# Key-1 quarters for the last add, the store and the maximum of a gate chunk

## The chip, the cores and the metric

One NeuronCore of a Trainium2 chip runs the whole program. The metric is the device time of one execution in microseconds, the median of several runs. The engines are named as in the profile: PE (matrix products), PEld (its weight loads), DVE (vector), ACT (scalar, which also has a DMA queue of its own, shown as ACTq), POOL (gather DMAs here), SP (the queue that loads weights).

## The reference, cut to what matters

Two transformer layers on 256 tokens of width 2048. The change lies in the first layer's expert stage: each token picks, for each of 8 heads, 16 of 16384 experts by two keys of 128, and mixes them.

```python
v1, i1 = lax.top_k(s1, 16)            # key 1: best 16 of 128, per token and head
v2, i2 = lax.top_k(s2, 16)            # key 2
cand = v1[..., :, None] + v2[..., None, :]
sc, sel = lax.top_k(cand.reshape(T, 8, 256), 16)
eidx = i1 * 128 + i2                  # of the selected pairs: 128 experts a token
gates = softmax(sc)
act = gelu(einsum('cd,ced->ce', x, u_emb[eidx]))
out = einsum('ce,ced->cd', gates * act, v_emb[eidx])
```

The kernel computes `act` densely for all 16384 experts, spreads the gates into a dense table by key 1, key 2 and token, and then reads the rows of both that some token uses.

## The kernel before, in words

**The dense products.** `linear` (L140) computes 512 output columns for all 256 tokens in two PSUM banks named `lin`. `wtile` loads 128x2048 weights (`raw`, three buffers, SP queue), `halves` splits each half of 1024 columns into a high part on ACT (`whi`, L123) and a rest on DVE (`wlo`, L124), four buffers of each, and `mm3` multiplies high by high (L134), rest by high (L135) and high by low (L136). A half feeds 12 matrix products. The stretch of interest is the product with `u`: 32 calls of `linear`, each followed by Gelu on ACT (`act`, L783), eight transposes on PE (L790), a copy (`actT`, L792) and two stores of 256 KB on ACT's queue (L794).

**The gate table.** Beside it runs the gate work, four chunks of 64 tokens (loop at L652). For each pair of tokens there are one-hot rows on DVE (L657 to L661) and ACT (L666), two products into a PSUM bank `sc` (L667, two banks), a copy of the high part on ACT (`gh`, L672) and an add on DVE into `gsb` (L673). `gsb` is 128 (key 2, partitions) x 128 (key 1) x 64 (tokens), and there is one buffer. When a chunk is full, ACT's queue issues two stores, each of 64 keys 1 (2 MB in runs of 64 floats, L676), and DVE takes the maximum over the 64 tokens in one instruction (L678, L681), which says what experts are used. The next chunk's first add must wait until the stores have landed.

**The order.** A scheduler places every engine's instructions in a fixed order by priorities. The gate work has a low priority, except what stands under `prompt()`, which has that of the dense products. After the four chunks come the places and lists (L700 to L774), still beside the product with `u`, and then the stage that gathers rows of `v` by these lists.

Of the kernel before, what the change touches and what calls it, by code (L numbers as in the profile page):

```python
# [12 lines left out]
F32 = mybir.dt.float32  # L13
# [5 lines left out]
ALU = mybir.AluOpType  # L19
AX = mybir.AxisListType  # L20

P = 128
# [34 lines left out]
def tile_kernel(ctx: ExitStack, tc: tile.TileContext, A, out):  # L57
    nc = tc.nc
    V, S, G, TE = nc.vector, nc.scalar, nc.gpsimd, nc.tensor

    def pool(name, bufs=1, space=None, stack=ctx):
        kw = {"space": space} if space is not None else {}
        return stack.enter_context(tc.tile_pool(name=name, bufs=bufs, **kw))
# [8 lines left out]
    def bank(name="bk"):  # L72
        tg, nb = {"lin": ("lin", 3), "tp": ("tp", 2), "sc": ("sc", 2), "z": ("sc", 2)}.get(name, ("x", 1))
        return pp.tile([P, 512], F32, tag=tg, name=name, bufs=nb)
# [286 lines left out]
    for c in range(2):  # L361
# [7 lines left out]
        for j in range(0, 4, 2):  # L369
# [9 lines left out]
            for jj in range(2):  # L379
                xh, xl = yl(4 * c + j + jj)  # L380
                split(y[:, jj, :], xh, xl, vcol("g_lru", 4 * c + j + jj))
                for tt in range(2):
# [4 lines left out]
                        axis=AX.X, op=ALU.add)  # L387
# [84 lines left out]
    for c in range(2):  # L472
        ps = linear(WIN, 5 + c, xt, range(4))
        qsb = []
        for tt in range(2):
            q = ap_.tile([P, 8, 64], F32, tag="qsb", name="qsb")
# [50 lines left out]
    AGv = AG.rearrange("(i p) (e a t) -> p i e a t", p=P, e=2, a=2)  # L527
# [22 lines left out]
    for n in range(4):  # L550
        ps = linear(A["w_pq"], n, x1t, range(4))
        qs = []
        for tt in range(2):
            q = rq.tile([P, 512], F32, tag="rq", name="rq", bufs=2)
# [22 lines left out]
    @contextmanager  # L577
    def prompt():

        low[0] = tc.cur_priority  # L580
        tc.cur_priority = low0
        yield
        tc.cur_priority = low[0]
# [9 lines left out]
    for tt in range(2):  # L593
# [23 lines left out]
        for half, op, c in ((0, ALU.logical_shift_right, 4), (1, ALU.bitwise_and, 15)):  # L617
# [5 lines left out]
            for h in range(8):  # L623
# [4 lines left out]
                                op=ALU.mult)  # L628
# [15 lines left out]
    gp = pool("gates", 1, stack=r3p)  # L644


    used = rp.tile([P, 2, P], F32, tag="used", name="used")
# [3 lines left out]
    for c in range(4):  # L651
        gsb = gp.tile([P, P, 64], F32, tag="gsb", name="gsb", bufs=1)  # L652
        for t0 in range(0, 64, 4):
            t = 64 * c + t0
            io = iota.unsqueeze(1).to_broadcast([P, 4, P])
            oh = gp.tile([P, 4, P], F32R, tag="oh2", name="oh2", bufs=2)
            V.tensor_tensor(oh, io, i2T[:, t:t + 4].unsqueeze(2).to_broadcast([P, 4, P]), op=ALU.is_equal)  # L657
            o1 = gp.tile([P, 4, P], F32, tag="oh1", name="oh1", bufs=2)
            V.tensor_tensor(o1, io, i1T[:, t:t + 4].unsqueeze(2).to_broadcast([P, 4, P]), op=ALU.is_equal)
            og = gp.tile([P, 4, 2, P], F32R, tag="og", name="og", bufs=2)  # L660
            V.tensor_tensor(og[:, :, 1, :], o1, gT[:, t:t + 4].unsqueeze(2).to_broadcast([P, 4, P]), op=ALU.mult)  # L661
            for k0 in range(0, 4, 2):
                ps = bank("sc")
                for k in range(k0, k0 + 2):
                    with prompt():
                        S.activation(og[:, k, 0, :], o1[:, k, :], AF.Copy, scale=gTh[:, t + k:t + k + 1])  # L666
                        TE.matmul(ps[:, (k - k0) * T:(k - k0 + 1) * T], lhsT=oh[:, k, :],  # L667
                                  rhs=og[:, k].rearrange("p a b -> p (a b)"), start=True, stop=True)
                pv = ps.rearrange("p (k m i) -> p m i k", k=2, m=2)
                gh = gp.tile([P, P, 2], F32, tag="gh", name="gh", bufs=2)  # L670
                with prompt():
                    S.activation(gh, pv[:, 0], AF.Copy)  # L672
                    V.tensor_tensor(gsb[:, :, t0 + k0:t0 + k0 + 2], gh, pv[:, 1], op=ALU.add)  # L673
        h, t0 = c // 2, c % 2 * 64
        for e in range(0, P, 64):
            S.dma_start(AGv[:, 1 + e:65 + e, h, 1, t0:t0 + 64], gsb[:, e:e + 64, :])  # L676
        if t0 == 0:
            V.tensor_reduce(used[:, h, :], gsb, axis=AX.X, op=ALU.max)  # L678
        else:
            um = gp.tile([P, P], F32, tag="um", name="um")  # L680
            V.tensor_reduce(um, gsb, axis=AX.X, op=ALU.max)  # L681
            V.tensor_tensor(used[:, h, :], used[:, h, :], um, op=ALU.max)
    r3p.close()

# [179 lines left out]
    last = []  # L864
# [14 lines left out]
    with tc.If(more > 0):  # L879
        with tc.For_i(0, P, 1) as k:  # L880
# [10 lines left out]
            for c in range(4):  # L891
# [5 lines left out]
                for tt in range(2):  # L897
# [5 lines left out]
                    op=ALU.mult)  # L903
# [102 lines left out]
    for h0 in (0, 4):  # L1006
        for tt in range(2):
            s = mq.tile([P, 4, T], F32, tag="s2", name="s2", bufs=2)
            for j in range(2):
# [3 lines left out]
                for hh in range(2):  # L1013
                    h = h0 + 2 * j + hh
# [80 lines left out]
    for h0 in (0, 4):  # L1095
        for tt in range(2):
# [4 lines left out]
            for e in range(2):  # L1101
                ps = bank("sc")
                b = slice(64 * e, 64 * e + 64)
                for j in range(2):
                    h = h0 + 2 * j + e
# [172 lines left out]
```

## Time and profile before

| | us |
|---|---|
| median of 3 runs | 3051.96 |
| lowest, highest run | 3048.44, 3052.6 |
| the profiled execution, its own time | 3049.11 |
| its span, first to last instruction | 3047.3 |
| PE busy in the span | 2970.9 (97%) |
| DVE busy | 2002.0 (66%) |
| ACT busy | 1576.9 (52%) |

PE is the engine whose queue is the program: what it does not wait for costs nothing. The times in the trace are counted from the start of the span. A row that begins with a time is one instruction, or several alike merged, with its start, its duration, and in brackets how long the engine sat idle before it and what ended that. ACTq rows are DMA issues, and their duration is the time that ACT's queue was held by the issue, not the time of the transfer. "issue" as a releaser means that the engine waited for nothing that the profile shows as work.

### The profile page before, as it was taken

The page shows a single profiled execution, that of the slowest core. Times are in us where ns is not written, and L with a number is a line of the kernel's source. Part 1 is how long each engine was busy: PE and PEld are TensorE (multiplying, and loading weights), DVE is VectorE, ACT ScalarE, POOL GpSimd, SP SyncE. Part 2 cuts the span into 40 slices and gives each one's busy share as a digit, 9 for nine tenths or more (in the row PEclk, how much of TensorE's full clock was granted, in tenths as well). Part 3 has the DMA queues.
Part 4 walks back from the last instruction along what each step waited for, and adds up shares of the span by engine and source line. Part 5 has one row for each costly group of instructions (what it writes and reads, how often), then busy time and mean ns, then how long its engine had stood idle before and what let it go on. Part 6 is the DMA issues. An engine that isn't in the chain of part 4 may idle for free. (4 is left out here: it accounts for less than half of the span.)

```text
span 3047.3 us, 36250 instructions
## 1 busy us (share of the span) xinstructions
PE 2970.9 (97%) x13729; PEld 2443.6 (80%) x13729; DVE 2002.0 (66%) x2944; ACT 1576.9 (52%) x2221; POOL 271.0 (9%) x232
## 2 busy tenths in 40 slices
PE   9999999998988999899999999999999999999999
PEld 7887888887877778678887788778888888888887
DVE  6885789877766769467777756664655454445454
ACT  6754545565655645455565555544444444344443
POOL 0000000000000000477662000000000000000000
PEclk9999999999999999999999999999999999999999
DMA  6442546656567575688886454554655555555554
GB/s 231 155 174 98 180 166 210 215 196 219 189 205 217 181 232 184 226 327 325 333 322 250 173 183 169 205 179 169 242 193 187 194 185 188 193 193 194 190 190 159
DMA packets 197168, 626.26 MB, mean 206 GB/s; under 512 B 82688, under 2 KB 116096, under 8 KB 129664
## 3 DMA queue, kind: packets, MB, share of 16 engines
q1 hardware_dynamic: 73728, 460.55, 42.8%
q0 software_dynamic: 20784, 124.79, 11.1%
q10 hardware_dynamic: 102480, 38.58, 4.8%
q8 instruction: 108, 1.77, 0.2%
q14 instruction: 68, 0.56, 0.1%
HBM read 583.77 MB, written 40.11 MB: 205 GB/s over the span
## 5 line engine op out<-in xcount | busy, mean ns | idle before, releaser
L124 DVE TENSOR_TENSOR wlo<-raw,whi 128x1024 fp32r<-128x1024 f32 (+1 forms) x972 | 1181.4, 1221 | 772.5 <-ACT whi L123 759.8
L123 ACT ACTIVATE whi<-raw 128x1024 fp32r<-128x1024 f32 (+1 forms) x972 | 1023.4, 1057 | 1087.0 <-PE lin L136 901.6
L134 PE MATMUL lin<-whi,x1th 128*128 128x512 f32 x1152 | 451.5, 399 | 25.4 <-ACT whi L123 25.4
L135 PE MATMUL lin<-wlo,x1th 128*128 128x512 f32 x1152 | 457.9, 397 | 6.2 <-DVE wlo L124 6.2
L136 PE MATMUL lin<-whi,x1tl 128*128 128x512 f32 x1152 | 457.1, 397 | 0.0
L134 PEld LDWEIGHTS lin<-whi,x1th 128*128 128x128 f32 x1152 | 219.6, 191 | 70.0 <-ACT whi L123 27.7
L136 PE MATMUL lin<-whi,x3tl 128*128 128x512 f32 x704 | 274.9, 391 | 0.0
L135 PE MATMUL lin<-wlo,x3th 128*128 128x512 f32 x704 | 274.2, 389 | 0.0
L134 PE MATMUL lin<-whi,x3th 128*128 128x512 f32 x704 | 269.5, 390 | 0.0
L135 PEld LDWEIGHTS lin<-wlo,x1th 128*128 128x128 f32 x1152 | 220.4, 191 | 51.3 <-DVE wlo L124 8.5
L136 PEld LDWEIGHTS lin<-whi,x1tl 128*128 128x128 f32 x1152 | 220.1, 191 | 43.5
L135 PE MATMUL lin<-wlo,y1th 128*128 128x512 f32 x512 | 200.7, 393 | 0.8 <-DVE wlo L124 0.8
L134 PE MATMUL lin<-whi,y1th 128*128 128x512 f32 x512 | 199.4, 395 | 1.7 <-ACT y1th L159 1.2
L136 PE MATMUL lin<-whi,y1tl 128*128 128x512 f32 x512 | 198.5, 393 | 0.8 <-DVE y1tl L160 0.8
L135 PEld LDWEIGHTS lin<-wlo,x3th 128*128 128x128 f32 x704 | 132.2, 188 | 27.3
L136 PEld LDWEIGHTS lin<-whi,x3tl 128*128 128x128 f32 x704 | 132.2, 188 | 27.1
L134 PEld LDWEIGHTS lin<-whi,x3th 128*128 128x128 f32 x704 | 132.2, 188 | 26.9
L130 POOL DMA_INDIRECT vag<-ag,idg x102 | 134.2, 1315 | 53.7 <-issue 26.5
L136 PE MATMUL lin<-whi,at 128*128 128x512 f32 x352 | 137.2, 390 | 0.0
L135 PE MATMUL lin<-wlo,at 128*128 128x512 f32 x352 | 137.0, 389 | 0.0
L134 PE MATMUL lin<-whi,at 128*128 128x512 f32 x352 | 135.5, 389 | 0.0
L134 PEld LDWEIGHTS lin<-whi,y1th 128*128 128x128 f32 x512 | 96.2, 188 | 22.4 <-ACT y1th L159 1.8
(440 smaller groups left out, 4750.1 us busy)
## 6 DMA issues: line engine op xcount, KB each, us to landing
raw<-in_u_dram SPq DMA_DIRECT2D x128, 1024.0 KB, 4.8
raw<-in_w_in_dram SPq DMA_DIRECT2D x91, 1024.0 KB, 4.8
raw<-in_w_gu_dram SPq DMA_DIRECT2D x88, 1024.0 KB, 4.8
raw<-in_w_dn_dram SPq DMA_DIRECT2D x44, 1024.0 KB, 4.7
raw<-in_w_out_dram SPq DMA_DIRECT2D x16, 1024.0 KB, 4.8
raw<-in_w_pq_dram SPq DMA_DIRECT2D x16, 1024.0 KB, 4.8
ag<-actT ACTq DMA_DIRECT2D x64, 256.0 KB, 3.0
ag<-gsb ACTq DMA_DIRECT2D x8, 2048.0 KB, 15.5
```

Source lines behind the costliest of these rows:

```text
L123: S.activation(h[:, q], r, AF.Copy)
L124: V.tensor_sub(l[:, q], r, h[:, q].bitcast(F32))
L130: G.indirect_dma_start(out=dst, out_offset=None, in_=src, in_offset=bass.IndirectOffsetOnAxis(ap=rows, axis=0))
L134: TE.matmul(ps, lhsT=xh, rhs=wh, start=start, stop=False)
L135: TE.matmul(ps, lhsT=xh, rhs=wl, start=False, stop=False)
L136: TE.matmul(ps, lhsT=xl, rhs=wh, start=False, stop=stop)
```

## The change

For the last two tokens of a chunk the add (until now one instruction of 128 keys under `prompt()`) is put off until after the loop and cut into four quarters of 32 keys 1. Behind each quarter's add stand, in the program, the store of that quarter (1 MB, all 64 tokens) and the maximum of that quarter, into `um`. In the chunks whose maximum went straight into `used`, a copy from `um` now follows. So a chunk has four adds of 64 columns, four stores and four maxima where it had one add of 256 columns, two stores and one maximum. The quarter adds, the stores and the maxima have the low priority.

```diff
                 with prompt():
                     S.activation(gh, pv[:, 0], AF.Copy)
-                    V.tensor_tensor(gsb[:, :, t0 + k0:t0 + k0 + 2], gh, pv[:, 1], op=ALU.add)
+                    if not last:
+                        V.tensor_tensor(gsb[:, :, t0 + k0:t0 + k0 + 2], gh, pv[:, 1], op=ALU.add)
...
-        for e in range(0, P, 64):
-            S.dma_start(AGv[:, 1 + e:65 + e, h, 1, t0:t0 + 64], gsb[:, e:e + 64, :])
+        um = gp.tile([P, P], F32, tag="um", name="um")
+        for e in range(0, P, 32):
+            q = slice(e, e + 32)
+            V.tensor_tensor(gsb[:, q, 62:64], gh[:, q], pv[:, 1, q], op=ALU.add)
+            S.dma_start(AGv[:, 1 + e:33 + e, h, 1, t0:t0 + 64], gsb[:, q, :])
+            V.tensor_reduce(um[:, q], gsb[:, q, :], axis=AX.X, op=ALU.max)
         if t0 == 0:
-            V.tensor_reduce(used[:, h, :], gsb, axis=AX.X, op=ALU.max)
+            V.tensor_copy(used[:, h, :], um)
         else:
-            um = gp.tile([P, P], F32, tag="um", name="um")
-            V.tensor_reduce(um, gsb, axis=AX.X, op=ALU.max)
             V.tensor_tensor(used[:, h, :], used[:, h, :], um, op=ALU.max)
```

The scheduler makes a new order from this. ACT at the end of the first chunk, before:

```order
L123 ACTIVATE whi<-raw 128x1024
L672 ACTIVATE gh<-sc 128x256
L676 DMA ag<-gsb 128x64x64 x2
L123 ACTIVATE whi<-raw 128x1024 x2
L672 ACTIVATE gh<-sc 128x256
L666 ACTIVATE og<-oh_4516,gTh 128x128 x4
L123 ACTIVATE whi<-raw 128x1024 x2
```

and now:

```order
L123 ACTIVATE whi<-raw 128x1024
L673 ACTIVATE gh<-sc 128x256
L682 DMA ag<-gsb 128x32x64 x4
L123 ACTIVATE whi<-raw 128x1024 x2
L673 ACTIVATE gh<-sc 128x256
L666 ACTIVATE og<-oh_4526,gTh 128x128 x4
L123 ACTIVATE whi<-raw 128x1024 x2
```

Two issues became four at one place, with nothing between them. DVE there likewise has its four adds in a row, a one-hot row, and then its four maxima in a row: the adds and maxima do not alternate. In the second chunk the four stores stand together too, where before the second store stood behind two stores of `actT` and one `whi`.

ACT at the end of the third chunk, before:

```order
L123 ACTIVATE whi<-raw 128x1024
L676 DMA ag<-gsb 128x64x64 x2
L123 ACTIVATE whi<-raw 128x1024
L672 ACTIVATE gh<-sc 128x256
L666 ACTIVATE og<-oh_5230,gTh 128x128 x4
L792 ACTIVATE actT<-tp 128x512 x2
L123 ACTIVATE whi<-raw 128x1024
L794 DMA ag<-actT 128x4x128 x2
L123 ACTIVATE whi<-raw 128x1024 x2
```

and now:

```order
L682 DMA ag<-gsb 128x32x64
L799 DMA ag<-actT 128x4x128 x2
L682 DMA ag<-gsb 128x32x64
L123 ACTIVATE whi<-raw 128x1024
L682 DMA ag<-gsb 128x32x64 x2
L123 ACTIVATE whi<-raw 128x1024
L673 ACTIVATE gh<-sc 128x256
L666 ACTIVATE og<-oh_5258,gTh 128x128 x4
L123 ACTIVATE whi<-raw 128x1024 x2
```

The pair of `actT` stores moved from behind the chunk's stores into their middle, and one `whi` stands between the second and the third quarter. In the fourth chunk the first quarter stands alone, then `act` and one `whi`, then three quarters.

PE at the beginning of the second chunk, before and now (a run of four `sc` products serves four tokens and fills two banks; `lin` is the dense product):

```order
L136 MATMUL lin<-whi,x1tl 128x512
L667 MATMUL sc<-og,oh_4492 128x256 x4
L667 MATMUL sc<-og,oh_4514 128x256 x4
L134 MATMUL lin<-whi,x1th 128x512 x2
L135 MATMUL lin<-wlo,x1th 128x512
```

```order
L136 MATMUL lin<-whi,x1tl 128x512
L667 MATMUL sc<-og,oh_4502 128x256 x4
L134 MATMUL lin<-whi,x1th 128x512 x2
L667 MATMUL sc<-og,oh_4524 128x256 x2
L135 MATMUL lin<-wlo,x1th 128x512
```

The second chunk began with eight such products in one run and now begins with four, the next ones spread out. The third chunk began with eight and now begins with twelve; the fourth began with twelve and now begins with eight.

## Rows read from the trace of the kernel before

**Rows 1.** Waits of PE from 700 to 1110: total us, times, longest.
```profile
PE lin L134 <- ACT whi L123: 25.4, 6, 7.6
PE lin L135 <- DVE wlo L124: 6.2, 5, 1.7
PE sc L667 <- DVE gsb L673: 5.9, 4, 1.7
```
**Rows 2.** Windows: length, busy us of PE, PEld, DVE, ACT, POOL (instructions), PEclk, DMA, GB/s.
```profile
640.00:690.00 50.00, 50.00 (x244) 42.02 (x243) 37.94 (x54) 34.38 (x70) 0.00 (x0) 1.00 0.54 190
829.00:872.00 43.00, 31.93 (x126) 25.19 (x126) 27.29 (x27) 17.43 (x32) 0.00 (x0) 0.84 0.79 220
```
**Rows 3.** Timeline of ACT and its DMA queue at the ends of the four chunks.
```profile
697.54 0.38 ACTq L676 DMA_DIRECT2D ag<-gsb  x1
697.95 9.98 ACTq L676 DMA_DIRECT2D ag<-gsb  x1
...
829.28 9.66 ACTq L794 DMA_DIRECT2D ag<-actT  x1
839.63 1.06 ACT L123 ACTIVATE whi<-raw 128x1024 fp32r<-128x1024 f32 x1 [9.57 <-issue]
...
960.07 9.37 ACTq L676 DMA_DIRECT2D ag<-gsb  x2
973.03 10.42 ACTq L794 DMA_DIRECT2D ag<-actT  x1
...
1087.12 11.12 ACTq L676 DMA_DIRECT2D ag<-gsb  x2
```
**Rows 4.** Timeline of PE there: the first products after a stop.
```profile
710.03 0.69 PE L134 MATMUL lin<-whi,x1th 128*128 128x512 f32 x1 [5.01 <-ACT whi L123]
...
844.07 0.80 PE L134 MATMUL lin<-whi,x1th 128*128 128x512 f32 x1 [7.55 <-ACT whi L123]
...
970.43 0.50 PE L135 MATMUL lin<-wlo,x1th 128*128 128x512 f32 x1 [1.26 <-DVE wlo L124]
985.22 0.79 PE L134 MATMUL lin<-whi,x1th 128*128 128x512 f32 x1 [6.79 <-ACT whi L123]
...
1100.35 0.79 PE L134 MATMUL lin<-whi,x1th 128*128 128x512 f32 x1 [5.28 <-ACT whi L123]
```
**Rows 5.** Windows behind two stops and inside a run of gate products.
```profile
710.10:713.00 2.90, 2.90 (x7) 2.31 (x8) 2.90 (x5) 2.26 (x6) 0.00 (x0) 0.51 0.96 218
844.10:849.80 5.70, 5.70 (x14) 4.44 (x15) 2.12 (x4) 0.64 (x1) 0.00 (x0) 0.50 1.14 348
731.80:737.40 5.60, 3.86 (x9) 2.79 (x10) 5.60 (x8) 4.50 (x9) 0.00 (x0) 0.70 0.17 37
```
**Rows 6.** Timeline of PE at the beginning of the second and the fourth chunk.
```profile
728.56 0.63 PE L667 MATMUL sc<-og,oh 128*128 128x256 f32 x4
730.91 0.83 PE L667 MATMUL sc<-og,oh 128*128 128x256 f32 x4 [1.72 <-DVE gsb L673]
734.26 0.80 PE L135 MATMUL lin<-wlo,x1th 128*128 128x512 f32 x1 [1.73 <-DVE wlo L124]
...
996.06 0.83 PE L667 MATMUL sc<-og,oh 128*128 128x256 f32 x4 [0.76 <-DVE gsb L673]
998.61 0.83 PE L667 MATMUL sc<-og,oh 128*128 128x256 f32 x4 [1.72 <-DVE gsb L673]
```
**Rows 7.** Timeline of DVE: last add and maximum of a chunk, next chunk's first add.
```profile
697.10 0.41 DVE L673 TENSOR_TENSOR gsb<-gh,sc 128x256 f32<-128x256 f32 x1
698.03 8.68 DVE L678 TENSOR_REDUCE used<-gsb 128x128 f32<-128x8192 f32 x1
...
726.59 0.75 DVE L673 TENSOR_TENSOR gsb<-gh,sc 128x256 f32<-128x256 f32 x2 [6.54 <-DMA ag<-gsb]
```
**Rows 8.** Timeline of ACT's queue: a pair of small stores with nothing ahead.
```profile
723.61 1.33 ACTq L794 DMA_DIRECT2D ag<-actT  x2
```
**Rows 9.** Timeline of POOL: the second gather of rows of `v`.
```profile
1237.51 0.94 POOL L130 DMA_INDIRECT raw<-in_v_dram,idv  x1 [12.24 <-DVE wlo L124]
```

More of the change, by code (lines that the diff above doesn't have):

```diff
@@ L670, in tile_kernel @@
                 gh = gp.tile([P, P, 2], F32, tag="gh", name="gh", bufs=2)
+                last = t0 + k0 == 62
                 with prompt():
                     S.activation(gh, pv[:, 0], AF.Copy)
-                    V.tensor_tensor(gsb[:, :, t0 + k0:t0 + k0 + 2], gh, pv[:, 1], op=ALU.add)
+                    if not last:
+                        V.tensor_tensor(gsb[:, :, t0 + k0:t0 + k0 + 2], gh, pv[:, 1], op=ALU.add)
         h, t0 = c // 2, c % 2 * 64
-        for e in range(0, P, 64):
-            S.dma_start(AGv[:, 1 + e:65 + e, h, 1, t0:t0 + 64], gsb[:, e:e + 64, :])
+        um = gp.tile([P, P], F32, tag="um", name="um")
[4 more added lines that the diff above has]
+            V.tensor_reduce(um[:, q], gsb[:, q, :], axis=AX.X, op=ALU.max)
         if t0 == 0:
-            V.tensor_reduce(used[:, h, :], gsb, axis=AX.X, op=ALU.max)
+            V.tensor_copy(used[:, h, :], um)
         else:
-            um = gp.tile([P, P], F32, tag="um", name="um")
-            V.tensor_reduce(um, gsb, axis=AX.X, op=ALU.max)
             V.tensor_tensor(used[:, h, :], used[:, h, :], um, op=ALU.max)
```

## The prediction

> **What bounds the kernel now.** I read first the waits of PE, since PE is busy for nearly the whole span. Between 700 and 1110, where the chunks of the gate table end, it waits 25.4 us for `whi` in 6 waits, 6.2 us for `wlo` and 5.9 us for the adds into `gsb` [rows 1]. The windows say that this is confined to the chunk ends: from 640 to 690 PE is busy throughout at granted clock 1.00; from 829 to 872 it is busy for 31.93 of 43.00 us and the mean clock is 0.84 [rows 2]. Third, the queue of ACT, since `whi` is ACT's work. At a chunk's end the first store of `gsb` holds ACT's queue for 0.38 us, and the next DMA behind it for 9.98 us [rows 3]. It need not be the second half: in the second chunk a small store of `actT` stands behind the first half and is held 9.66 us, in the third one stands behind the second half and is held 10.42 us [rows 3]. So what holds ACT is that a large store issued earlier on this queue is still being worked off; its own issue is free, and whoever comes next pays. ACT makes no `whi` meanwhile, and PE stops for 5.01, 7.55, 1.26 and 6.79 (third chunk, twice) and 5.28 us [rows 4]. After a stop it runs some microseconds at the lower of its two levels, 1.2 GHz: 5.70 us at 0.50 in the second chunk, 2.90 us at 0.51 in the first [rows 5]. DVE's maximum of 8.68 us [rows 7] runs inside the same hold.
>
> **The change, hold first.** The bytes and runs of a chunk's stores are the same, so a quarter store is half of a half store. Holds behind a half store, from its issue: 0.38 and 9.98 with a gap give 10.4 us in the first chunk, some 10 in the second (9.66 and the first half's own issue), 9.37 in the third, 11.12 in the fourth [rows 3]. Half of that is 4.7 to 5.6 us, 5.1 in the mean. Before, a chunk's two halves cost one such hold; the last piece of a run is free. Four quarters cost three: 14.1 to 16.7 us, 5.1 more than now. This rests on holds going with the size of what lies ahead; a pair of `actT` stores of 256 KB takes 1.33 us for both issues [rows 8], against 10 behind 2 MB, which supports it.
>
> The rows also meet a rule. Here a DMA issue took 9.98 us of ACT's queue. The Trainium skill (DMA: Bandwidth & Descriptors, Issuing engines are not separate DMA queues) says that the sequencer time to initiate a DMA is usually small beside the DMA itself; by it the cut costs eight short issues and nothing more. What that would give here is the first rival.
>
> *First chunk.* The order around the stores is otherwise the same, and PE stops at the same product. The stop of 5.01 grows by half of 10.4: +5.2. A longer stop was followed by a longer stretch at half clock; from 2.90 to 5.70 us of it is +1.4 us of PE time [rows 5].
>
> *Second chunk.* The four stores stand together. Now PE stops at 836.5 (844.07 less 7.55 [rows 4]), 7 us after ACT was caught, and resumes 4.4 us after ACT's first `whi` at 839.63 [rows 3], since the product at its head needs the third `whi`, behind `gh` and four one-hot rows. In the new order the head is a transpose of `act`, which stands behind `whi`, `gh`, four one-hot rows, `whi` and `act`: about the same 4.4 us. So 3 x 5.1 + 4.4 - 7 = 12.7 in place of 7.55: +5.1, less a little for a longer run-up: +4.7.
>
> *Third chunk.* Before, two holds, and PE stopped for 1.26 and 6.79, 8.05 together. Now one chain: first quarter, the pair of `actT`, second quarter, one `whi`, two quarters: 3 x 4.7 + 1.3 = 15.4 us. PE's queue has here a run of three L134 products, the third of which belongs to the next column block and needs the third `whi` from there, behind all quarters, `gh` and the one-hot rows (it is the pattern of the second chunk before). 15.4 + 4.4 - 6.8 = 13.0: +5.0.
>
> *Fourth chunk.* From the last gate product to the product that stops, the order counts 54 dense products now and 46 before. At 0.2 us each (14 in 5.70 us at half clock [rows 5]) that is 1.8 us more cover, and PE resumes at the first `whi`, not the second, 1.1 us sooner. Three quarters at 4.7 to 5.1 hold 14.1 to 15.3 us, 3.0 to 4.2 more than the 11.12 of now; less 2.9 that is 0.1 to 1.3, taken +0.7; with quarters of 5.6 it would be 2.8.
>
> **Gate products at the chunk starts.** Eight in a row make PE wait 1.72 us for the second four (a bank is free only after DVE's add), then 1.73 for `wlo` [rows 6], and the window behind has clock 0.70 over 5.60 us, 1.7 us [rows 5]: 5.2 in all. The start with twelve shows one wait more, 0.76 and 1.72 [rows 6]. So a third run of four costs about 2.5 with its clock. The second chunk goes from eight to four: 0 to -5.2, taken -3.4, since `whi` still comes late there. The third goes from eight to twelve, +2.5; the fourth from twelve to eight, -2.5.
>
> **What is hidden.** An add of 256 columns takes 0.41 us [rows 7]; four of 64 take between 0.4 and 1.6, taken 0.8. Four maxima take 8.68 and a little for three more starts. The copy is a fraction of a microsecond. All this lies inside a hold of 14 us and more; if the hold were short, it would cost the 1 us or so on DVE per chunk. The first store is issued a few tenths earlier, which is all that the turn-taking brings, as all adds are queued ahead of all maxima and the maxima free nothing for the stores. The gate work ends later in PE's order, and so do the lists; POOL's second gather waits 12.24 us for a weight buffer and not for the list [rows 9], which covers a shift of about 12 us.
>
> **The sum.** First chunk 5.2 + 1.4 - 3.4 = 3.2, second with the third's start 4.7 + 2.5 = 7.2, third with the fourth's start 5.0 - 2.5 = 2.5, fourth 0.7: +13.6 us on the profiled execution's 3049.11 gives 3062.7. The median of the runs is 2.9 above that execution, the runs spread over 4.2; with half of it I forecast 3064.
>
> **Rivals.** *The hold does not grow.* If the queue took several quarters at once, ACT would be held about 10 us a chunk as now. Then the first chunk gives -3.4, the second +2.5, the third 10 + 1.3 + 4.4 - 6.8 = 8.9 for 8.05 and -2.5, the fourth about -2: -4.5, 3044.6, or 3047 against the median; with the whole -5.2 and less DVE time 3043. For it: sizes of 1 MB were not seen behind each other on this queue. Against it: even a 256 KB store was held the full 9.66 us. The rule of the Trainium skill above would give this.
>
> *The runs of gate products vanish.* While ACT is held, weight buffers stay full and SP loads nothing, so the store has the DMA engines to itself for 15 us, not 10, and lands sooner. The next chunk's first add, which waited 6.54 us for the landing [rows 7], starts at once, and all three bursts (5.2, 5.2, and 7.7 for the twelve) go: -18.1 in place of my -3.4, so the sum is 13.6 - 14.7 = -1.1, 3048 to 3051. Against it: PE reached its gate products only at 728.56 [rows 6], after the landing at 726.59; and the fourth chunk began as badly without any such wait.
>
> *The hold grows by more.* In the second chunk a weight buffer now becomes free right at the stores, as it did in the first and fourth, where the holds were the longest (10.4 and 11.12 against 9.37). That, and the `actT` pair of the fourth chunk caught behind the last quarter, add 1 to 2 us each, 5 to 6 with the clock: 3070. It decides where loads fall into the hold.
>
> **How the numbers follow.** A measurement of this kernel can tell about 0.2%, 6 us, from no change: 3046 to 3058 is the same. My forecast has a chance of 0.56, the greater hold 0.14, the vanished runs 0.14, the unchanged hold 0.16. Of the forecast's own spread (the -5.2 to 0 at the second chunk, 0 to 2.8 at the fourth, a run-up of 1 us) a small part falls below 3058. Slower 0.69; same 0.23, from the vanished runs and half of the unchanged hold; faster 0.08. The range reaches from the unchanged hold's median to past the greater hold: 3047 to 3073.
>
> **What would show it.** Right: three ACTq rows of L682 of 4.5 to 5.6 us each in a chunk, ACT idle "issue" of 14 to 17 us; PE stops of about 10, 12, 13 and 6 us; landings sooner than now; window clock lower at these places; twelve gate products at the third chunk's start with two waits. Wrong: if the second and third quarters issue in 0.4 us, the hold is not by size, and the first rival holds; if PE's stops stay near 5 to 8 us with ACT held for 15, PE had more `whi` ahead than I count.

## The result, and the profile after

The changed kernel takes 3065.76 us (median of 6 runs, 3062.57 to 3070.01), the kernel before beside it 3050.57 (3048.44 to 3052.6): a ratio of 1.0051 with a 95% interval of 1.0038 to 1.0064, or 15.2 us more. The forecast was 3064. The spans of the two profiled executions are 3047.3 and 3060.8 us, 13.5 apart.

Where the time went is told by the stretch from 690 to 1150, which holds the chunk ends and starts: in these 460 us PE was busy for 422.32 us before and 406.31 after, 16.0 less, and did 1936 and 1857 products, at mean granted clocks of 0.96 and 0.93. Up to 690 PE is busy for 678.97 us before and 678.65 after, with 3261 and 3271 products, so little changed ahead of it; behind 1150 it idles for 27.4 and 25.9 us, so a little comes back.

The waits of PE from 690 to 1150 in the changed kernel (total us, times, longest). They answer to [rows 1], which hold all that PE waits in this stretch of the kernel before:

```profile
PE lin L134 <- ACT whi L123: 33.3, 6, 14.6
PE tp L795 <- ACT act L788: 12.3, 2, 11.7
PE sc L667 <- DVE gsb L675: 5.3, 3, 1.8
PE lin L135 <- DVE wlo L124: 2.6, 4, 1.4
```

The first two are the same wait: `act` stands behind `whi` on ACT, and in the second chunk the product at the head of PE's queue is a transpose of `act`. Together 45.6 us, against 25.4. The wait for `wlo` fell from 6.2 to 2.6. In all PE waits 53.5 us where it waited 37.5: 16.0 more, which is the busy time that it lost.

ACT and its DMA queue at the ends of the four chunks, to be held against [rows 3] (start, duration, count, idle time before and its releaser):

```profile
695.83 0.38 ACTq L682 DMA_DIRECT2D ag<-gsb  x1
696.25 14.88 ACTq L682 DMA_DIRECT2D ag<-gsb  x3
711.17 2.00 ACT L123 ACTIVATE whi<-raw 128x1024 fp32r<-128x1024 f32 x2 [14.67 <-issue]
...
836.25 16.17 ACTq L682 DMA_DIRECT2D ag<-gsb  x4
852.52 1.06 ACT L123 ACTIVATE whi<-raw 128x1024 fp32r<-128x1024 f32 x1 [15.21 <-issue]
...
971.38 4.05 ACTq L799 DMA_DIRECT2D ag<-actT  x1
976.36 0.87 ACTq L682 DMA_DIRECT2D ag<-gsb  x1
977.36 12.49 ACTq L682 DMA_DIRECT2D ag<-gsb  x2
989.90 1.06 ACT L123 ACTIVATE whi<-raw 128x1024 fp32r<-128x1024 f32 x1 [11.51 <-issue]
...
1109.66 4.12 ACTq L682 DMA_DIRECT2D ag<-gsb  x1
1113.82 10.76 ACTq L682 DMA_DIRECT2D ag<-gsb  x2
1124.68 1.06 ACT L123 ACTIVATE whi<-raw 128x1024 fp32r<-128x1024 f32 x1 [13.43 <-issue]
1126.73 4.48 ACTq L799 DMA_DIRECT2D ag<-actT  x2
```

The first quarter issues in 0.38 us, and each DMA behind a quarter is held for 4.1 to 7.5 us, whether it is a quarter or a small `actT` store (971.38); a quarter behind small stores is not (976.36, 0.87 us). Three held issues make 14.88 us in the first chunk, 4.05 and 12.49 in the third. The last row is the pair of `actT` stores behind the fourth chunk's last quarter: there it is a fourth hold.

PE's stops, to be held against [rows 4]:

```profile
713.22 0.80 PE L134 MATMUL lin<-whi,x1th 128*128 128x512 f32 x1 [9.71 <-ACT whi L123]
...
856.58 0.69 PE L795 MATMUL tp<-ident,act 128*128 128x128 f32 x2 [11.73 <-ACT act L788]
...
993.38 0.80 PE L134 MATMUL lin<-whi,x1th 128*128 128x512 f32 x1 [14.57 <-ACT whi L123]
...
1125.79 1.22 PE L134 MATMUL lin<-whi,x1th 128*128 128x512 f32 x2 [3.70 <-ACT whi L123]
...
1144.56 1.15 PE L134 MATMUL lin<-whi,x1th 128*128 128x512 f32 x2 [3.30 <-ACT whi L123]
```

The last of these is not a hold's. The `actT` pair's hold ends at 1131.2, and PE does not wait from 1125.79 to 1139.8. ACT there:

```profile
1131.32 2.01 ACT L123 ACTIVATE whi<-raw 128x1024 fp32r<-128x1024 f32 x2 [3.67 <-PE lin L135]
1138.28 0.69 ACT L788 ACTIVATE act<-lin,r 128x512 f32<-128x512 f32 x1 [4.95 <-PE lin L136]
...
1143.45 2.00 ACT L123 ACTIVATE whi<-raw 128x1024 fp32r<-128x1024 f32 x2 [1.40 <-issue]
```

In the new order the next `whi` stand behind two `act`, two `actT` and a pair of short stores, so ACT first waits 4.95 us for PE, and then PE for ACT: 0.56 us for `act` and 3.30 for `whi`. The kernel before has no such wait behind its last chunk. Four more runs of the changed program have it, of 0.56 and 2.97 us: half stores, not in turn, eighths, and quarters on SP, where no store of `gsb` stands on ACT's queue at all.

What the quarters do on DVE and in the queue, from the view of the tile `gsb` between 690 and 1130 (ns: least, median, greatest), and the time to landing in us:

```profile
L681 DVE TENSOR_TENSOR gsb<-gh,sc x16: 215/218/223, 695.6 to 1109.3; 128x64 f32<-128x64 f32 x16
L682 ACTq DMA_DIRECT2D ag<-gsb x16: 378/4510/7524, 695.8 to 1118.6; - x16
L683 DVE TENSOR_REDUCE um<-gsb x16: 2277/2282/2285, 696.7 to 1116.0; 128x32 f32<-128x2048 f32 x16
DMA to landing us min/median/max: 6.2/11.8/14.7
```

In a row four adds take 0.61 us and four maxima 8.87; in before the maximum took 8.68 [rows 7]. The stores land sooner (the first chunk's last piece at 718.3, where it was 726.5), and DVE no longer waits for them, where the first add of the second chunk waited 6.54 us [rows 7].

### The profile page after: what moved, and what is told of

Same layout as the page of the kernel before. It is cut to its first block, busy times and chain, and to the rows that moved or that the text cites. A ratio compares the mean times of both kernels' runs of the same rounds, so it can differ in the third digit from the quotient of the medians.

```text
span 3060.8 us, 36290 instructions
## 1 busy us (share of the span) xinstructions
PE 2969.1 (97%) x13729; PEld 2441.7 (80%) x13729; DVE 2003.1 (65%) x2970; ACT 1577.1 (52%) x2221; POOL 268.9 (9%) x232
## 6 DMA issues: line engine op xcount, KB each, us to landing
ag<-gsb ACTq DMA_DIRECT2D x16, 1024.0 KB, 11.8
```

## The experiments

All were timed in five rounds beside the kernel before, whose median was 3050.2 to 3050.5 us. Theory: a DMA issue on ACT's queue is held until the large store ahead of it on that queue is worked off, in proportion to what lies ahead, and PE runs dry behind it. The table gives PE's products and mean clock in the 460 us from 690 on.

| kernel | us | ratio, 95% interval | products | clock |
|---|---|---|---|---|
| before | 3050.5 | 1 | 1936 | 0.96 |
| the change | 3065.76 | 1.0038 to 1.0064 | 1857 | 0.93 |
| quarter stores alone | 3060.77 | 1.0024 to 1.0052 | 1883 | 0.94 |
| the change with half stores | 3057.05 | 1.0012 to 1.0030 | 1905 | 0.94 |
| the same, not in turn | 3054.96 | 1.0006 to 1.0024 | 1896 | 0.93 |
| eighths | 3078.04 | 1.0075 to 1.0106 | 1833 | 0.93 |
| stores of 16 and 112 keys | 3052.26 | 0.9997 to 1.0015 | 1917 | 0.95 |
| the change, stores on POOL | 3054.08 | 1.0002 to 1.0020 | 1909 | 0.94 |
| side tile | 3060.45 | 1.0021 to 1.0045 | 1918 | 0.94 |
| side tile, halves on POOL | 3059.86 | 1.0020 to 1.0042 | 1919 | 0.94 |
| halves on SP | 3025.64 | 0.9911 to 0.9940 | 2074 | 0.97 |
| the change, quarters on SP | 3024.35 | 0.9902 to 0.9930 | 2064 | 0.98 |

**One part alone: quarter stores.** The kernel before, its adds and maxima as they were:

```diff
-        for e in range(0, P, 64):
-            S.dma_start(AGv[:, 1 + e:65 + e, h, 1, t0:t0 + 64], gsb[:, e:e + 64, :])
+        for e in range(0, P, 32):
+            S.dma_start(AGv[:, 1 + e:33 + e, h, 1, t0:t0 + 64], gsb[:, e:e + 32, :])
```

> The kernel before with one thing changed: the two half stores of a chunk are cut into four quarter stores; one add and one maximum as before. Theory of the hold: three issues of 4 to 5.5 us each held in a chunk, about 15 us, PE's stops 4 to 5 us longer, 3060 to 3070 us. Rival (DVE's pieces and the moved order cost the time): no change, 3048 to 3053.

3060.77 us, 10.3 over the kernel before. ACT's queue at the first two chunk ends, and PE's wait for `whi` from 690 to 1150:

```profile
697.31 9.95 ACTq L676 DMA_DIRECT2D ag<-gsb  x2
707.33 4.74 ACTq L676 DMA_DIRECT2D ag<-gsb  x1
...
837.48 13.24 ACTq L676 DMA_DIRECT2D ag<-gsb  x3
```
```profile
PE lin L134 <- ACT whi L123: 36.1, 6, 14.6
```

The cut of the stores alone brings three holds of about 5 us and two thirds of the loss. The split adds and the turn-taking are not needed for it.

**The change without that part: half stores.** The adds and maxima stay in quarters:

```diff
-            S.dma_start(AGv[:, 1 + e:33 + e, h, 1, t0:t0 + 64], gsb[:, q, :])
+            if e % 64 == 32:
+                S.dma_start(AGv[:, e - 31:33 + e, h, 1, t0:t0 + 64], gsb[:, e - 32:e + 32, :])
```

> The changed kernel with one thing undone: quarter adds and quarter maxima stay, but a chunk is stored in two halves again. Theory (an issue on ACT's queue waits until the large store ahead of it is worked off, so a chunk costs the holds of all pieces but the last): one hold of about 10 us a chunk in place of 15 to 16, PE's stops at the chunk ends some 5 us shorter in the first three chunks and 2 to 4 in the fourth, about 3050 us (3046 to 3054). Rival (the cut adds and maxima on DVE, their lower priority and the gate products that moved in PE's order cost the time): it stays at 3062 to 3068.

3057.05 us: 8.7 of the 15.2 come back, which lies between the two expectations. What remains is seen on ACT in the fourth chunk:

```profile
1108.70 12.91 ACTq L800 DMA_DIRECT2D ag<-actT  x2
1121.71 2.00 ACT L123 ACTIVATE whi<-raw 128x1024 fp32r<-128x1024 f32 x2 [12.09 <-issue]
```

In the kernel before this pair is issued ahead of the stores (at 1082.66, 1.40 us); here it stands behind the second half. So it is the same hold, with another instruction caught, and PE's stop there is 7.28 us in place of 5.28. The other part of what remains is the order's stop of 0.56 and 2.97 us behind it, which is no hold. The two parts, 10.3 and 6.6, make 16.9 where the change has 15.2.

**Not in turn.** As the last, with all four adds first, then the two stores, then the maxima; the edit is against the change.

```diff
             V.tensor_tensor(gsb[:, q, 62:64], gh[:, q], pv[:, 1, q], op=ALU.add)
-            S.dma_start(AGv[:, 1 + e:33 + e, h, 1, t0:t0 + 64], gsb[:, q, :])
+        for e in range(0, P, 64):
+            S.dma_start(AGv[:, 1 + e:65 + e, h, 1, t0:t0 + 64], gsb[:, e:e + 64, :])
+        for e in range(0, P, 32):
+            q = slice(e, e + 32)
             V.tensor_reduce(um[:, q], gsb[:, q, :], axis=AX.X, op=ALU.max)
```

> The changed kernel with two half stores again, and with all four quarter adds first, then the stores, then the four quarter maxima: the quarters stay, but no store waits for a maximum. Beside the half stores in turn (3057.05) it tells what 'in turn' costs. If the rest of 6.6 us over the kernel before came from the second store's issue standing behind maxima (the actT pair of the fourth chunk held behind it, 6.9 us later than the adds): 3047 to 3053. If it came from the split adds and maxima themselves or from another order that they bring: 3055 to 3060.

3054.96 us, at the border of the two. The trace decides for the order: the `actT` pair of the fourth chunk is again behind the last half (held 12.76 us, where the pair with nothing ahead took 1.33 [rows 8]), and the order's second stop is there too. Whether taking turns costs the 2 us between this and the last run, the intervals do not tell.

**A larger dose: eighths.** The change with steps of 16 keys in place of 32.

```diff
-        for e in range(0, P, 32):
-            q = slice(e, e + 32)
+        for e in range(0, P, 16):
+            q = slice(e, e + 16)
...
-            S.dma_start(AGv[:, 1 + e:33 + e, h, 1, t0:t0 + 64], gsb[:, q, :])
+            S.dma_start(AGv[:, 1 + e:17 + e, h, 1, t0:t0 + 64], gsb[:, q, :])
```

> The changed kernel with eighths of key 1 in place of quarters: eight stores of 0.5 MB a chunk. If what is held is all that lies ahead of the last piece, the hold grows from 3/4 to 7/8 of some 20 us, by 2.5 us a chunk, and the split costs DVE four more adds and maxima: 3068 to 3080, about 3073. Rival: a piece small enough is not held (the queue takes the next issue once little is left of the one ahead, and the maxima of 1.1 us between two issues give it time): 3045 to 3060.

3078.04 us, inside the range and above its middle: the smaller pieces are held too, and for longer than expected. In the first chunk seven held issues take 20.8 us, 5.9 more than the quarters' three and not 2.5. PE's longest waits from 690 to 1150 are 16.0 and 17.5:

```profile
697.02 8.02 ACTq L682 DMA_DIRECT2D ag<-gsb  x3
705.16 12.75 ACTq L682 DMA_DIRECT2D ag<-gsb  x4
```
```profile
PE lin L134 <- ACT whi L123: 36.5, 4, 16.0
PE tp L795 <- ACT act L788: 17.5, 1, 17.5
```

**A small first store.** The kernel before with stores of 16 and of 112 keys, so that little lies ahead of the second.

```diff
-        for e in range(0, P, 64):
-            S.dma_start(AGv[:, 1 + e:65 + e, h, 1, t0:t0 + 64], gsb[:, e:e + 64, :])
+        for e, f in ((0, 16), (16, P)):
+            S.dma_start(AGv[:, 1 + e:1 + f, h, 1, t0:t0 + 64], gsb[:, e:f, :])
```

> The kernel before with the same two stores a chunk, but uneven: 16 keys first, 112 keys second; the order on ACT is that of before. Theory of the hold: the second issue waits only for the 16 keys, 1.3 to 3 us in place of 10, so the stops at the ends of the first, second and fourth chunk nearly go; in the third chunk the small stores of actT come 13 us behind the large store and are held some 5 to 9 us, a stop of 3 to 6 us stays. About 3026 us (3020 to 3040). Rival (the hold goes with the number of stores, or the DMA engines are what PE waits for): as before, 3047 to 3054.

3052.26 us: no gain, and the expectation of 3026 missed. The time is the rival's, but not for the rival's first reason: the hold did go with the size ahead (3.35 us). Now the next chunk's first add waits longer. ACT, then DVE, then PE's waits from 690 to 1150:

```profile
698.23 3.35 ACTq L676 DMA_DIRECT2D ag<-gsb  x1
701.63 2.01 ACT L123 ACTIVATE whi<-raw 128x1024 fp32r<-128x1024 f32 x2 [3.36 <-issue]
```
```profile
698.31 8.68 DVE L678 TENSOR_REDUCE used<-gsb 128x128 f32<-128x8192 f32 x1
...
728.33 0.76 DVE L673 TENSOR_TENSOR gsb<-gh,sc 128x256 f32<-128x256 f32 x2 [11.90 <-DMA ag<-gsb]
```
```profile
PE sc L667 <- DVE gsb L673: 14.8, 6, 5.1
PE lin L135 <- DVE wlo L124: 14.0, 9, 2.7
PE lin L134 <- ACT whi L123: 11.2, 4, 6.8
```

The waits of PE moved from `whi` (25.4 to 11.2) to `sc` and `wlo` (12.1 to 28.8). ACT's hold had covered two other things. One is the landing: with ACT free sooner DVE is ready for the next chunk's first add at 716.4 in place of 720.05 [rows 7], but the store lands no sooner, at 728.3 and not 726.6. In the second chunk, too, DVE is ready 3.2 us sooner and the wait grows from 6.75 to 12.13. The other is DVE's maximum of 8.68 us, since DVE works in order and `wlo` stands behind it: PE waits 2.67, 1.50 and 1.72 us for `wlo` behind the maxima of the first, second and fourth chunk, which is 5.9 of the 7.8 us by which that wait grew. The last 1.89 come behind the first instruction of the lists, which waits 12.78 us for the last landing.

**Stores on POOL's queue.** The change with the quarters issued by POOL, so that ACT is held by none.

```diff
-            S.dma_start(AGv[:, 1 + e:33 + e, h, 1, t0:t0 + 64], gsb[:, q, :])
+            G.dma_start(AGv[:, 1 + e:33 + e, h, 1, t0:t0 + 64], gsb[:, q, :])
```

> The changed kernel, but its four quarter stores a chunk are issued on POOL's queue, where nothing else stands in this stage. Theory of the hold: ACT is not held at all, PE stops only 1 to 3 us at a chunk's end for wlo behind DVE's four maxima, about 3030 us (3020 to 3042). Rival (DVE's pieces and order): 3060 to 3066. A second rival (the transfers themselves, late landings): the next chunk's first add waits for the landing for 10 us and more and DVE's queue behind it, 3045 to 3075.

3054.08 us, as the second rival said. PE waits 0.7 us for `whi` in all, yet the same landing takes the place (waits from 700 to 1110):

```profile
DVE gsb L675 <- DMA ag<-gsb: 44.2, 3, 15.2
PE sc L667 <- DVE gsb L675: 23.8, 6, 7.0
```

PE also waits 18.4 us for `wlo`: 3.06 behind the first chunk's maxima, and 7.92 in one piece at 1128.00, behind the first instruction of the lists, which waits 14.43 us for the last landing.

**A side tile against the landing wait.** In the kernel before, the first 12 tokens of a chunk go into a small tile that POOL copies into `gsb` later; once with the stores where they were, once with the halves on POOL (`G` in place of `S`).

```diff
-        gsb = gp.tile([P, P, 64], F32, tag="gsb", name="gsb", bufs=1)
+        gs0 = gp.tile([P, P, 12], F32, tag="gs0", name="gs0", bufs=1)
...
-                    V.tensor_tensor(gsb[:, :, t0 + k0:t0 + k0 + 2], gh, pv[:, 1], op=ALU.add)
+                    to = gs0 if t0 < 12 else gsb
+                    V.tensor_tensor(to[:, :, t0 + k0:t0 + k0 + 2], gh, pv[:, 1], op=ALU.add)
+            if t0 == 8:
+                gsb = gp.tile([P, P, 64], F32, tag="gsb", name="gsb", bufs=1)
+                G.tensor_copy(gsb[:, :, 0:12], gs0)
```

> Kernel before with the side tile of 12 tokens alone; the half stores stay on ACT's queue. Theory: the hold of ACT (9.4 to 11.1 us a chunk) stays and with it PE's stops of 7 to 8 us at the chunk's end; only the landing wait (DVE 13.3 us in 2, of which PE saw 5.9 us) goes: 3040 to 3051, about 3046. Rival: the landing was the true bound in before and the hold cost nothing by itself: 3020 to 3035.

> Kernel before with two edits: the two half stores are issued on POOL's queue, so ACT is held by none; and the first 12 tokens of each chunk are added into a small side tile, which POOL copies into gsb after the 12th token, so that DVE's first adds no longer wait for the landing of the chunk before. If hold and landing are the two things that bound a chunk's end in turn, both fall: ACT's whi wait of 25.4 us and DVE's landing wait of 13.3 us go, and with them most of the 8.9 us that PE lost at a chunk's end and half of the 8 to 9 us at its start, in three chunks, and some clock: 3010 to 3035, about 3025. Rival: one moves the stop once more (POOL's copy waits for a store that the weight loads slow, for longer than 12 tokens take, some 20 us, and the adds behind it wait, or the copy slows DVE): 3045 to 3065, with DVE waiting for POOL at the 13th token.

3060.45 and 3059.86 us. The first missed both its cases: the landing wait is gone, but the schedule changed with it. The gate work ended 30 us earlier (last add at 1057.1), and the fourth chunk's `actT` pair now stands behind the last half. ACT there, and a window at the second chunk's start, where DVE is the bound:

```profile
1067.62 10.15 ACTq L798 DMA_DIRECT2D ag<-actT  x2
```
```profile
854.50:870.00 15.50, 9.80 (x32) 6.88 (x30) 15.03 (x23) 11.80 (x30) 1.47 (x1) 0.69 0.29 92
```

These are not enough to account for it: PE's waits in the 460 us grew by 2.5 us only, from 37.5 to 40.0, so most of the 10 us is not placed. What the landing wait cost by itself in the kernel before is therefore open. The second went as its rival: POOL's copy of the second chunk, and with it the 13th token's add, had to wait until 731.8 for halves issued from 698.2 on, and PE waited 27.0 us for `sc` and 20.7 for `wlo`, 12.5 of these behind the lists' first instruction, which waits for the last landing.

**Stores on SP's queue.** The halves of the kernel before, and then the quarters of the change, issued between the weight loads.

```diff
-            S.dma_start(AGv[:, 1 + e:65 + e, h, 1, t0:t0 + 64], gsb[:, e:e + 64, :])
+            nc.sync.dma_start(AGv[:, 1 + e:65 + e, h, 1, t0:t0 + 64], gsb[:, e:e + 64, :])
```

> Kernel before with the two half stores of each chunk on SP's queue, between the weight loads, in place of ACT's. Theory: a queue that issues behind a large store is held for it whichever queue it is, so the some 10 us of hold move to SP; there only the next weight loads stand behind the second half, and PE has three raw tiles of loaded weights in hand (6 whi tiles of 12 products at 0.4 us, some 29 us), so the hold is covered; and since the loads stand still meanwhile, the store lands undisturbed, in 20 to 22 us. ACT's whi wait of 25.4 us goes, and the landing wait stays as in the kernel before: 3020 to 3038, about 3028. Rival: the loads that are held come late (the raw tiles are drained while the store takes the DMA engines), and PE waits on whi for a load in place of the store: 3045 to 3070.

> The changed kernel with its quarter stores on SP's queue. If what a quarter costs is the hold of the queue that issues it, and SP's hold of 14 to 17 us is covered by the loaded weights as one of 10 us is, it lies within 6 us of the half stores on SP: 3020 to 3040. Rival: the loads stand still for 15 us or more and the raw tiles run dry, so that it is 8 us or more above the half stores on SP: 3040 to 3065, with PE waiting for whi and whi for a raw load.

3025.64 and 3024.35 us: both are faster than either kernel, by 25 and 26 us against before and by 40 and 41 against the change. SP's queue at the first chunk's end with halves, then at the first two with quarters:

```profile
700.49 10.46 SPq L676 DMA_DIRECT2D ag<-gsb  x2
711.92 25.69 SPq L113 DMA_DIRECT2D raw<-in_u_dram  x4
```
```profile
696.55 15.35 SPq L682 DMA_DIRECT2D ag<-gsb  x4
...
829.72 16.96 SPq L682 DMA_DIRECT2D ag<-gsb  x4
```

PE's waits from 690 to 1150, of the quarters on SP:

```profile
PE lin L135 <- DVE wlo L124: 8.3, 7, 3.0
PE lin L134 <- ACT whi L123: 5.8, 4, 3.0
PE sc L667 <- DVE gsb L675: 5.2, 3, 1.7
```

The holds are as long as on ACT: 10.46 for halves, 15.35 and 16.96 for quarters. But behind them stand only weight loads, for which PE has the next tiles in hand; how far that cover reaches no run tested (the expectation's 29 us count 0.4 us a product, while products at full clock start 0.23 us apart). With halves on SP the wait for `whi` falls to 1.8 us, that for `wlo` grows from 6.2 to 10.8, for the most part behind the maxima, and that for `sc` stays at 5.9. That last is the difference to POOL and to the uneven stores. Counted from the second chunk's first issue, DVE is ready for the next add sooner here too, after 16.9 us in place of 22.6; but the loads stand behind the store on the same queue, and the store lands sooner as well, after 23.2 us in place of 29.4. With quarters the longest stop falls from 14.6 to 3.0 us, and that one is for `wlo`, behind the four maxima. The same cut into quarters that costs 15 us on ACT's queue costs nothing here that the runs can tell.

## Why the prediction was right, point by point

- **The hold.** Forecast: three holds of 4.7 to 5.6 us a chunk, 14.1 to 16.7 in all. Measured: 14.88, 16.17, 16.54 (4.05 and 12.49) and 14.88 (4.12 and 10.76). That the hold is what costs most is shown from three sides: quarters alone bring it, eighths more of it, and on SP's queue the same quarters are free. Not all of the 15.2 us is the hold's: the new order's stop behind the fourth chunk, 3.9 us of waits, comes with it or without.
- **First chunk.** The stop was to be 10.2 us and was 9.71. The stretch at 1.2 GHz behind it was forecast as 5.70 us and was some 4.9: PE's products stay at 0.63 us each from 713.8 to 718.1, and the window shows clock 0.50:

```profile
714.00:718.00 4.00, 4.00 (x11) 3.12 (x10) 3.69 (x6) 1.55 (x4) 0.00 (x0) 0.50 1.03 213
730.00:737.00 7.00, 5.25 (x25) 3.94 (x24) 3.88 (x6) 4.12 (x10) 0.00 (x0) 1.00 0.03 9
```

- **The second chunk's start.** Fewer gate products in a row were to save 3.4 us. In the second of these windows the clock stays at 1.00, where it was 0.70 [rows 5], and the two waits of 1.72 and 1.73 [rows 6] became 1.18 and 0.57: 1.7 of waits and 1.7 of clock. Here the size was right.
- **Second chunk.** Forecast 12.7, measured 11.73 us; the head of PE's queue is the transpose, as foreseen. Of the twelve gate products at the third chunk's start two waits of 1.72 were seen, as forecast. The third wait, for `wlo`, shrank from 1.43 to 0.19, and all waits there came to 3.63 us for 3.52 before, so the 2.5 us taken for them were too much.
- **Third chunk.** Forecast 13.0, measured 14.57. The mis-sized term is the last two quarters: 12.49 us for two issues, 4.93 and 7.52, where 4.7 each was taken from the shorter hold of [rows 3]. That is 3.1 us more, of which half came back, since PE stopped later and went on sooner than counted. And the 1.26 us in the 8.05 before was no stop for ACT's hold: its row names `wlo`, which stands behind DVE's maximum. So the stop that the hold makes grew from 6.79 to 14.57, and that wait went.
- **Fourth chunk.** Here the step failed, twice. The main stop was to grow by 0.7 us and shrank from 5.28 to 3.70, with 0.40 before it: the cover was mis-sized, since PE ran on for 12.4 us after ACT was caught (1109.7 to 1122.1) where it had run 7.5 (1087.5 to 1095.1), and I had taken 1.8 more. And the second stop, of 0.56 and 3.30 us, was put at nothing, though it lies in the new order: it is what `act` and `actT` ahead of the next `whi` cost. Together 7.96 us of waits against 5.28, or +2.7 in place of +0.7, before the clock.
- **The sum.** The stops grew by 4.7, 4.2, 6.5 and 2.7 us, 18.1 together, where 5.2, 4.7, 5.0 and 0.7, or 15.6, were forecast. Of the starts, the third chunk's took less than the 2.5 forecast, and the fourth's gave back less: one wait for the adds of 1.83 us in place of 0.76 and 1.72 [rows 6], 0.65 where 2.5 with the clock were taken, and the waits for `whi` and `wlo` beside it grew by 0.47. The span grew by 13.5 for 13.6 forecast. Errors of 1 to 4 us of both signs cancelled; that the total is so much closer than its terms is luck.
- **What was hidden.** The adds took 0.61 us for an estimate of 0.8, the maxima 8.87. PE waits behind them once, the 0.40 us above. The lists end later by more than was allowed for: the first gather of rows of `v` starts at 1247.70 and not 1222.48. As PE is later too, the gather of [rows 9] still waits for a weight buffer, but 1.36 us and no longer 12.24: it cost nothing, with little to spare.
- **The rivals.** The unchanged hold is out: the median issue took 4.51 us. With it goes, for this queue, what the Trainium skill (DMA: Bandwidth & Descriptors, Issuing engines are not separate DMA queues) says of a usually small time to initiate: 4.51 us stand here beside 11.8 to landing, and the measurement decides. The vanished bursts came true in part, at the second chunk only, where the new order alone had forecast it; the landing wait did go as that rival said. Of the greater hold, the `actT` pair was caught, for 4.48 us, but PE did not wait for it.

Some of my later expectations were worse than the prediction. For the uneven stores I counted what ACT's hold cost and not what ran beside it: DVE's maximum and the landing, which PE then waited for instead.

## What to carry to other kernels

Look at whose queue issues a large store: on ACT's and SP's queue here its cost was the time for which the next issue was held, so ask who stands behind that. Cutting the store into pieces lengthened the hold (all pieces but the last), and moving it to a queue whose next instructions had buffers in hand made it free. When a hold goes away, ask at once what it had covered: here a maximum on an engine that works in order, and a landing behind a single buffer. And read a new order to its end: one stop of this change came from the order alone.

## What was not expected of the hardware

- The hold is not ACT's own: SP's queue was held 10.46 us behind the first half and 15.35 us over four quarters, like ACT's.
- A store's landing is no fixed time. From the first issue of the first chunk's stores to the landing of the last, halves on SP took 22.1 us and quarters on ACT 22.5 (695.8 to 718.3), halves on ACT 29.0, and quarters on POOL 33 (697.4 to 730.4). That weight loads beside the store slow it fits with the first number, where they wait behind it; no run separates them from POOL's own part in the last.
- An issue on POOL takes POOL itself: 1.69 us for a quarter and 2.76 for a half, in the medians.
